# Four transpose banks, rotated running sums and two earlier weight requests in a decoder block's feed-forward part

## The chip, the core and the metric

The kernel runs on one core of a Trainium2 chip. The metric is device time in microseconds (us) for one execution; the median of three runs of the kernel before is 844.78 us. Engines are named as in the profile: PE (TensorE, matmuls and transposes), ACT (ScalarE), DVE (VectorE), POOL (GpSimd) and SP (SyncE, which only issues DMA transfers here). Each works through its own list of instructions in the order written; semaphores hold an instruction back until what it reads is ready and what it overwrites has been read. POOL has little to do in the part that is changed: two tiny powers and one load.

## The reference, cut to what matters

One decoder layer on 512 positions of width 1024. The part that the change touches is the end of sub-layer 1, the norm that follows, and the SwiGLU feed-forward part (`D_FF` = 2816):

```python
x = x + gate1 * (merged @ w_out)

h2 = rms_norm(x, norm2_g) * (1.0 + scale2) + shift2
f_g, f_u = jnp.split(h2 @ w_ffn_in, 2, axis=-1)
x = x + gate2 * ((jax.nn.silu(f_g) * f_u) @ w_ffn_out)
return rms_norm(x, final_norm_g)
```

## The kernel before, in words

Everything is float32 and split in two: a value is kept as a rounded part `hi` and a remainder `lo`, and a product is three matmuls (`mm3`, lines 51 to 55: hi*hi, hi*lo, lo*hi). So each block of weights that comes from HBM into a buffer called `raw` is copied by ACT to `hi` (line 110) and then subtracted by DVE to give `lo` (line 114); when DVE is done, the `raw` buffer is free and SP may ask for the next block. There are three `raw` buffers (`RAWB`), used in turn. All instructions are written out by hand in one order; no scheduler moves them.

**The output projection** (lines 1240 to 1278). The 512 positions are worked on in two halves of 256 (`half`). Half 0 goes through the eight blocks of `w_out`, `n_` = 0 to 7, with sums in PSUM banks 4 to 7; half 1 goes through the same blocks with sums in banks 0 to 3. When a 512-column half of the width is complete (`kts[0] == 6`, at `n_` = 3 and `n_` = 7 in half 1), `resid` (line 1101) multiplies by the gate, adds the residual (DVE) and sums the squares (ACT). Beside half 1's matmuls stand the norm of half 0 and the preparation of the first feed-forward blocks `WF0[0]` to `WF0[3]` (the first two for the gate, the last two for the up projection), which are asked for by `ensure`.

**The norm's transposes** (`norm2_T`, line 1130). The normed rows `xn` are transposed by PE, four 128x128 transposes into one PSUM bank (tile `x2T`, line 1152). One bank holds two 128-wide slices `kt` of the width, a pair `k2`; a half has four pairs. Each slice is read out of the bank twice, once by ACT (line 1159, gives `hi`) and once by DVE or ACT (lines 1162 and 1164, gives the unrounded `hf`), and DVE subtracts the two (line 1165, gives `lo`). The readers of one bank take turns. The pairs use banks 4 and 7 in turn. For half 0 the pairs (0, 1) are transposed after `n_` = 2 and the pairs (2, 3) after `n_` = 3; for half 1 two pairs stand behind each of the two blocks of the up projection of half 0 (line 1476).

**The first feed-forward groups** (lines 1464 to 1487) are plain products into banks 0 to 3 (tile `pf`): for half 0 the gate and then the up block, for half 1 the same. Beside them DVE forms differences of the normed halves (`t_diff`, line 1319) and ACT and DVE split these (`t_split`, line 1327).

**The half groups** (lines 1496 to 1568). The other groups are computed by a Strassen-like scheme with seven products instead of eight. A step `q` (from -2 to 17) handles half a group, gate for even `q` and up for odd. Its weights come in two blocks, asked for by `s_issue(q)` (line 1174) and worked into sums, `hi` and `lo` by `s_prep(q)` (four pairs of an ACT and a DVE part, `a0`,`d0` to `a3`,`d3`, lines 1205 to 1236). The weights of `q` are prepared while PE computes `q - 1`; those of `q` = -2 are prepared in the output projection (line 1269) and around it. `sprod` (line 1490) is one of the seven products, 12 matmuls of 256 columns, and adds to one of four PSUM tiles `R[0]` to `R[3]`. Between products ACT copies one running sum into the next bank (`R[1]` from `R[0]`, line 1529; `R[2]` from `R[1]`, line 1540) or out to `ps` (lines 1536 and 1547). Even `q` use banks 4 to 7 and odd `q` banks 0 to 3.

**The last product** (`zprod`, line 1591) does the same on the output weights with 512 columns, in the banks of the list `ZB`.

SP's list of transfers around the change is: the blocks of `w_out`, the four blocks `WF0`, then the two blocks of each half group from `q` = -2 on. Which buffer a block gets decides how long SP waits before it asks; and as SP's list is in order, a transfer that waits holds up all behind it.

Of the kernel before, what the change touches and what calls it, by code (L numbers as in the profile page):

```python
# [9 lines left out]
F32 = mybir.dt.float32  # L10
# [18 lines left out]
def block_kernel(ctx: ExitStack, tc: tile.TileContext, x, positions, w_ada, b_ada, w_in,  # L29
# [12 lines left out]
    def bank(k, name="bank"):  # L42
        return psum.tile([128, 512], F32, name=name, tag=f"b{k}", bufs=1)

    def f(ap):
        return ap.bitcast(F32)
# [11 lines left out]
    stream, wseq, chunk = [], [], {}  # L58
# [58 lines left out]
    def ensure(upto):  # L117
        upto = min(upto, len(stream) - 1, st["limit"] - 1)
        while True:
            for i in range(st["prep"], min(st["prep"] + 16, len(stream), st["limit"])):  # L120
                if "raw" in stream[i]:
                    continue
                if room(i):
                    issue(i)
                elif stream[i]["kind"] == "w" or not stream[i]["mid"]:
                    break
            if st["prep"] > upto:
                break
            prep(st["prep"])
            st["prep"] += 1  # L130

    def room(i):
        e = stream[i]
        pend = stream[st["prep"]:i]
        if e["kind"] == "m" and e["early"]:
            return sum(p["kind"] == "m" for p in pend) < 8
        if e["kind"] == "m" and e["mid"]:
            return all(p["kind"] == "w" for p in pend) and len(pend) <= 1
        return sum(p["kind"] == "w" or not (p["early"] or p["mid"]) for p in pend) < RAWB


    def get(i, ahead=2):
        k = wseq.index(i)
        ensure(wseq[min(k + ahead, len(wseq) - 1)])
        return chunk[i]
# [13 lines left out]
    ffn = []  # L159
# [114 lines left out]
    for i in range(4):  # L274
        t = base.tile([128, D], F32, name=f"x{i}", tag=f"X{i}", bufs=1)
# [30 lines left out]

    R = mid.tile([128, 6, 128], F32, name="ropes", tag="A1", bufs=1)
    posf, ang, nh, nl, t0 = R[:, 0], R[:, 1], R[:, 2], R[:, 3], R[:, 4]
    chain = []
# [168 lines left out]
    for kt in range(8):  # L478
        hi, lo = chunk[W1[kt]]
# [327 lines left out]
    for g in range(4):  # L807
        pb = [bank2(b, "pav") for b in nbanks()]
        for i in W_AV[g]:
# [10 lines left out]
            hi, lo = get(i)  # L820
# [306 lines left out]
            else:  # L1127
                V.tensor_scalar(xn[tk], xt[tk], r2[:, tk:tk + 1], None, op0=OP.mult)

    def norm2_T(half, kts, after=()):  # L1130
        if kts[0]:
            pass
        elif half == 0:
            for kh in range(2):
                t = ffn[0].tile([128, 4, 256], F32, name="h2f", tag=f"F{kh}", bufs=1)
                for j in range(4):
                    h2f[kh * 4 + j, 0] = t[:, j]
                h2f["t", kh, 0] = [t[:, 0:2], t[:, 2:4]]
        else:
            for kh in range(2):  # L1140
                h2f["t", kh, 1] = []
                for q in range(2):
                    t = base.tile([128, 2, 256], F32, name="h2f", tag=f"S1_{kh * 2 + q}", bufs=1)
                    h2f["t", kh, 1].append(t)
                    for j in range(2):
                        h2f[kh * 4 + q * 2 + j, 1] = t[:, j]
        for k2 in kts:
            p = bank(7 if k2 % 2 else 4, "x2T")
            for k in range(2):
                kt = k2 * 2 + k  # L1150
                for e in range(2):
                    T.transpose(p[:, k * 256 + e * 128:k * 256 + (e + 1) * 128],
                                xn[2 * half + e][:, kt * 128:(kt + 1) * 128], ident)
            for k in range(2):
                kt = k2 * 2 + k
                g, s = Gc[:, 1, kt:kt + 1], Gc[:, 1, 8 + kt:9 + kt]
                src = p[:, k * 256:(k + 1) * 256]
                hi, lo = (t[:, kt % 4] for t in HB[kt // 4, half])
                A.activation(hi, src, AF.Identity, scale=g, bias=s)  # L1159
                hf = h2f[kt, half]  # L1160
                if kt % 4 == 3 or half and kt % 2:
                    A.activation(hf, src, AF.Identity, scale=g, bias=s)  # L1162
                else:
                    V.tensor_scalar(hf, src, g, s, op0=OP.mult, op1=OP.add)  # L1164
                V.tensor_sub(lo, hf, f(hi))
            if k2 in after:
                for fn in after[k2]:
                    fn()


    NQ = 18
# [2 lines left out]
    def s_issue(q):  # L1174
        if q >= NQ:
            return
        c0 = (2 + q // 2) * 256 + (DFF if q % 2 else 0)
        sraw[q] = []
        for kh in range(2):
            if q > 0 and q % 2 and kh:  # L1180
                t = ffn[0].tile([128, 4, 2, 128], F32, name="raw", tag="F0", bufs=1)
            else:
                t = base.tile([128, 4, 2, 128], F32, name="raw", tag="raw", bufs=RAWB)
            SY.dma_start(t.rearrange("p j a n -> p j (a n)"),
                         w_ffn_in[kh * 512:(kh + 1) * 512, c0:c0 + 256].rearrange("(j p) n -> p j n", p=128))
            sraw[q].append(t)
# [53 lines left out]
    WF0 = W_F[0] + W_F[1]  # L1240
    OORD = (W_O, [W_O[n_] for n_ in (0, 2, 4, 5, 1, 3, 6, 7)])
    for half in range(2):
        po = {}
        for n_, (h, i) in enumerate(OORD[half]):
            if half == 0:
                wch[i] = get(i, min(4, 7 - n_))
            hi, lo = wch[i]
            kts = stream[i]["kts"]
            if kts[0] == 0:
                po[h] = [bank(4 - 4 * half + 2 * h + e, "po") for e in range(2)]  # L1250
            for e in range(2):
                opt_a_mm(po[h][e], 2 * half + e, hi, lo, kts, mT, 8)
            if kts[0] == 6:
                for e in range(2):
                    resid(po[h][e], 512 * h, 512, h, 2 * half + e, gate_b[1])
            if half == 1:
                if n_ == 1:
                    for e in range(2):
                        row_rstd(e)
                    norm2_x(0)  # L1260
                    ensure(WF0[1])
                if n_ in (2, 3):
                    norm2_T(0, (0, 1) if n_ == 2 else (2, 3))
                if n_ in (3, 4):
                    ensure(WF0[n_ - 1])
                if n_ == 4:
                    s_issue(-2)
                if n_ == 6:
                    pre = s_prep(-2)
                    for fn in pre[0]:  # L1270
                        fn()
# [47 lines left out]
    def t_diff():  # L1319
        for q in range(2):  # L1320
            b11, b21, b12, b22 = (h2f["t", kh, th][q] for th in range(2) for kh in range(2))
            V.tensor_sub(b11, b12, b11)
            V.tensor_sub(b12, b22, b12)
            V.tensor_sub(b22, b22, b11)
            V.tensor_sub(b21, b21, b22)
# [139 lines left out]
    for half in range(2):  # L1465
        o = slice(half * 256, (half + 1) * 256)
        for w in range(2):
            for ci, i in enumerate(W_F[w]):
                hi, lo = chunk[i]
                for j, kt in enumerate(stream[i]["kts"]):  # L1470
                    for m in range(2):
                        cc = slice(m * 128, (m + 1) * 128)
                        mm3(pf[w][m][:, o], (hi[:, j, cc], lo[:, j, cc]), tuple(t[:, j] for t in HB[ci, half]),
                            kt + half == 0, kt == 7, skip_group_check=True)
                if half == 0 and w == 1:
                    norm2_T(1, (2 * ci, 2 * ci + 1), {3: pre[3]})
            if half == 0 and w == 1:
                s_issue(-1)
                t_diff()
            if half == 1:  # L1480
                if w == 0:
                    EV[w](0)(pf[w])
                t_split(w + 1)
                if w == 1:
                    t_split(3)
                    EV[w](0)(pf[w])
                    t_split(4)
# [8 lines left out]
    for q in range(-2, NQ):  # L1496
# [3 lines left out]
        pre = s_prep(q + 1)  # L1500
        half_of = lambda t, e: tuple(v[:, :, e] for v in t)
        S2_, S1_, A12, A22, S4_, S3_ = (half_of(d[k], e) for k in "CBD" for e in range(2))
        R = [bank(k + 4 * (q % 2 == 0), "R")[:, :256] for k in range(4)]
        ps = [ffn[0].tile([128, 256], F32, name="ps", tag="rt", bufs=2) for _ in range(2)]
        if q >= NQ - 2:
            z_issue(("B11", "B12")[q - NQ + 2])
# [20 lines left out]
        pre[0][0]()  # L1527
        sprod(R[0], d["A"], HB[0, 0], True)
        A.activation(R[1], R[0], AF.Copy)  # L1529
        pre[0][1]()  # L1530
        while left:
            left.pop(0)()
        if q == NQ - 1:
            z_issue("B21")
        sprod(R[3], S1_, TB[1], True)
        A.activation(ps[0], R[3], AF.Copy)
        pre[1][0]()
# [48 lines left out]
            q.dma_start(out[tk * 128:(tk + 1) * 128, c], xo[tk][:, c])  # L1586


    Z, ZB = {}, ((4, 7), (5, 6), (1, 2), (0, 3))

    def zprod(k, ka, kw, start):
        if start:
# [83 lines left out]
    for h in range(2):  # L1676
# [4 lines left out]
        for n_, i in enumerate(ids[:-3] if h else ids):  # L1681
            kts = stream[i]["kts"]
            if h == 0:
                g_split(2 * n_ + 2)
            hi, lo = get(i)
# [91 lines left out]
```

## Time and profile before

| what | value |
|---|---|
| time, median of three runs (range) | 844.78 us (844.73 to 845.04) |
| profiled execution: its own time | 845.55 us |
| profiled execution: span from first to last instruction | 843.4 us |
| granted TensorE clock, mean | 0.997 |
| DVE busy in the span | 668.2 us (79%) |
| ACT busy in the span | 403.7 us (48%) |
| POOL busy in the span | 118.3 us (14%) |
| HBM read | 105.9 MB, 128 GB/s over the span |

Positions are given in us from the start of the span. The part around the change runs from about 470 (end of the output projection) to 532 (the second half group). In the profile an instruction is named by engine, source line and tile: "PE x2T L1152" is a transpose, "DVE h L1165" the subtraction that makes the `lo` part of a normed slice, "ACT wx L110" the copy of a feed-forward block to `hi`, "DVE raw L1212" the first sum over the weights of a half group, "PE R" a product of a half group. Busy time of PE is not a measure of what it could do, since its matmuls overlap; its idle time is.

### The profile page before, as it was taken

What the parts mean: (1) busy time and instruction counts of PE and PEld (TensorE: products, weight loads), DVE (VectorE), ACT (ScalarE), POOL (GpSimd) and SP (SyncE); (2) the same over time, 40 slices, a digit from 0 to 9 for tenths busy, and PEclk for the clock granted to TensorE, in tenths of its full rate; (3) what the DMA queues carried; (4) which work ended last, traced back from release to release, by engine and by line L of the source; (5) the groups of instructions that cost most, each with busy time, mean ns of one, the idle gap of its engine ahead of it and who ended that gap; (6) DMA issues with size and microseconds to landing.
All of it is one profiled execution on the core that took longest, in us unless ns stands there. A gap on an engine that the chain in (4) does not pass through costs nothing. (4 is left out here: it accounts for less than half of the span.)

```text
span 843.4 us, 12878 instructions
## 1 busy us (share of the span) xinstructions
PE 826.0 (98%) x4992; PEld 734.1 (87%) x4992; DVE 668.2 (79%) x1157; ACT 403.7 (48%) x706; POOL 118.3 (14%) x105
## 2 busy tenths in 40 slices
PE   7999999999999999999999989999999999999996
PEld 6788989988888888988888789999999999888885
DVE  7978799788899548886766678889999888985635
ACT  6664445332332226666333456555555555573322
POOL 2060022353344411002210000000000000000001
PEclk9999999999999999999999999999999999999998
DMA  9972362432345641036544130445553334143212
GB/s 297 300 198 68 98 199 77 126 89 86 109 144 197 197 152 51 26 114 236 175 149 150 51 100 26 127 152 162 168 163 108 100 100 146 56 141 99 85 50 100
DMA packets 95677, 109.09 MB, mean 129 GB/s; under 512 B 5617, under 2 KB 76273, under 8 KB 95617
## 3 DMA queue, kind: packets, MB, share of 16 engines
q1 hardware_dynamic: 92512, 101.37, 39.3%
q0 software_dynamic: 2384, 6.10, 2.0%
q8 instruction: 39, 0.64, 0.3%
q10 hardware_dynamic: 720, 0.82, 0.3%
q14 instruction: 22, 0.17, 0.1%
HBM read 105.90 MB, written 2.10 MB: 128 GB/s over the span
## 5 line engine op out<-in xcount | busy, mean ns | idle before, releaser
L110 ACT ACTIVATE hi<-raw 128x1024 fp32r<-128x1024 f32 (+2 forms) x83 | 85.6, 1035 | 107.2 <-PE pfo L55 35.4
L114 POOL TENSOR_TENSOR lo<-raw,hi 128x1024 fp32r<-128x1024 f32 x33 | 83.1, 2522 | 213.2 <-ACT hi L110 194.8
L114 DVE TENSOR_TENSOR lo<-raw,hi 128x1024 fp32r<-128x1024 f32 (+2 forms) x43 | 53.3, 1243 | 50.8 <-ACT hi L110 50.7
L53 PE MATMUL pb<-h,hi 128*128 128x512 f32 x192 | 76.5, 398 | 0.0
L55 PE MATMUL pb<-h,lo 128*128 128x512 f32 x192 | 75.8, 395 | 0.0
L54 PE MATMUL pb<-hl,hi 128*128 128x512 f32 x192 | 75.8, 395 | 0.0
L55 PE MATMUL pfo<-hi,gs 128*128 128x512 f32 (+1 forms) x126 | 46.5, 369 | 0.0
L54 PE MATMUL pfo<-lo,gs 128*128 128x512 f32 (+1 forms) x126 | 46.5, 369 | 0.0
L53 PE MATMUL pfo<-hi,gs 128*128 128x512 f32 (+1 forms) x126 | 46.4, 368 | 0.0
L53 PE MATMUL R<-tb,sx 128*128 128x256 f32 x160 | 45.3, 283 | 0.5 <-ACT R L1529 0.5
L53 PE MATMUL R<-tb,hi 128*128 128x256 f32 x160 | 45.1, 282 | 0.8 <-ACT ps L1547 0.7
L54 PE MATMUL R<-tb,sx 128*128 128x256 f32 x160 | 45.1, 282 | 0.0
L55 PE MATMUL R<-tb,sx 128*128 128x256 f32 x160 | 45.1, 282 | 0.0
L55 PE MATMUL R<-tb,lo 128*128 128x256 f32 x160 | 44.9, 280 | 0.0
L54 PE MATMUL R<-tb,hi 128*128 128x256 f32 x160 | 44.7, 279 | 0.0
L55 PEld LDWEIGHTS pb<-h,lo 128*128 128x128 f32 x192 | 36.0, 188 | 8.7
L54 PEld LDWEIGHTS pb<-hl,hi 128*128 128x128 f32 x192 | 36.1, 188 | 8.3
L53 PEld LDWEIGHTS pb<-h,hi 128*128 128x128 f32 x192 | 36.1, 188 | 8.2
L175 DVE SCALAR_TENSOR_TENSOR acc<-mraw,cols,acc 128x512 f32<-128x512 f32 x38 | 31.4, 826 | 9.4 <-DMA mraw<-in_w_ada_dram 8.6
L54 PE MATMUL pav<-lo,h 128*128 128x256 f32 x128 | 35.8, 280 | 0.0
L55 PE MATMUL pav<-hi,hl 128*128 128x256 f32 x128 | 35.8, 280 | 0.0
L53 PE MATMUL pav<-hi,h 128*128 128x256 f32 x128 | 35.8, 280 | 0.0
(376 smaller groups left out, 2655.3 us busy)
## 6 DMA issues: line engine op xcount, KB each, us to landing
raw<-in_w_ffn_in_dram SPq DMA_DIRECT2D x44, 512.0 KB, 4.1
raw<-in_w_in_dram SPq DMA_DIRECT2D x40, 512.0 KB, 3.8
mraw<-in_w_ada_dram SPq DMA_DIRECT2D x22, 512.0 KB, 3.9
raw<-in_w_ffn_out_dram SPq DMA_DIRECT2D x17, 512.0 KB, 3.8
s<-in_w_ada_dram SPq DMA_DIRECT2D x30, 256.0 KB, 5.5
raw<-in_w_ada_dram SPq DMA_DIRECT2D x10, 512.0 KB, 4.8
raw<-in_w_proj_a_dram SPq DMA_DIRECT2D x8, 512.0 KB, 4.7
raw<-in_w_proj_b_dram SPq DMA_DIRECT2D x8, 512.0 KB, 3.6
```

Source lines behind the costliest of these rows:

```text
L53: T.matmul(o, wh, rh, start=start, stop=False, **kw)
L54: T.matmul(o, wh, rlo, start=False, stop=False, **kw)
L55: T.matmul(o, wlo, rh, start=False, stop=stop, **kw)
L110: A.activation(hi[:, :m], e["raw"][:, :m], AF.Copy)
L114: e["lo"].tensor_sub(lo[:, :m], e["raw"][:, :m], f(hi[:, :m]))
L175: V.scalar_tensor_tensor(o, w, cs[:, j:j + 1], o, op0=OP.mult, op1=OP.add)
```

## The change

- `norm2_T` uses four banks, 4 + `k2`, and has lost the `after` argument.
- Half 0: all four pairs are transposed after `n_` = 2. The block `WF0[2]` is converted by ACT between pair 1 and pair 2, and its `lo` part by DVE between pair 2 and pair 3; the first two blocks of half group -2 are asked for there. `WF0[3]` follows after `n_` = 3, behind that step's `resid`.
- Half 1: all four pairs are transposed after the first of the two up blocks; the last part of the preparation of half group -2 (`pre[3]`) stands behind them.
- The second block of half group -1 goes into tile `E5`, which holds the first gate block until half 1 has used it, and no longer into a `raw` buffer. So the two blocks of half group 0 fall on `raw` buffers that come free sooner. Its issue is written behind the gate products of half 1.
- The running sums `R` use the banks 4, 1, 0, 7 for even `q` and 5, 2, 3, 6 for odd `q`; `ZB` is changed to match. Which sums share a bank with which earlier reader stays the same between half groups; for `q` = -2 and -1 the banks of `pf` and `x2T` come in instead.

The instructions are the same in number, except that PE's transposes stand in two runs of sixteen instead of four runs of eight.

```diff
-    def norm2_T(half, kts, after=()):
+    def norm2_T(half, kts):
...
-            p = bank(7 if k2 % 2 else 4, "x2T")
+            p = bank(4 + k2, "x2T")
...
-            if k2 in after:
-                for fn in after[k2]:
-                    fn()
...
-            if q > 0 and q % 2 and kh:
-                t = ffn[0].tile([128, 4, 2, 128], F32, name="raw", tag="F0", bufs=1)
+            if q % 2 and kh:
+                t = ffn[0].tile([128, 4, 2, 128], F32, name="raw", tag="F0" if q > 0 else "E5", bufs=1)
...
-                if n_ in (2, 3):
-                    norm2_T(0, (0, 1) if n_ == 2 else (2, 3))
-                if n_ in (3, 4):
-                    ensure(WF0[n_ - 1])
-                if n_ == 4:
+                if n_ == 2:
+                    stream[WF0[2]]["lo"] = "later"
+                    norm2_T(0, (0, 1))
+                    ensure(WF0[2])
+                    norm2_T(0, (2,))
+                    stream[WF0[2]]["do"]()
                     s_issue(-2)
+                    norm2_T(0, (3,))
+                if n_ == 3:
+                    ensure(WF0[3])
...
-                if half == 0 and w == 1:
-                    norm2_T(1, (2 * ci, 2 * ci + 1), {3: pre[3]})
+                if half == 0 and w == 1 and ci == 0:
+                    norm2_T(1, range(4))
+                    for fn in pre[3]:
+                        fn()
             if half == 0 and w == 1:
+                t_diff()
+            if half == 1 and w == 0:
                 s_issue(-1)
-                t_diff()
...
-        R = [bank(k + 4 * (q % 2 == 0), "R")[:, :256] for k in range(4)]
+        R = [bank(k, "R")[:, :256] for k in ((4, 1, 0, 7), (5, 2, 3, 6))[q % 2]]
...
-    Z, ZB = {}, ((4, 7), (5, 6), (1, 2), (0, 3))
+    Z, ZB = {}, ((4, 7), (0, 1), (2, 3), (5, 6))
```

## The prediction, made before the run

> **What bounds the kernel now.** First the list of PE's own waits, from 470 us on: engine, line, releaser, then total us, times, longest.
>
> ```profile
> PE x2T L1152 <- ACT h2f L1162: 2.1, 2, 1.4
> PE x2T L1152 <- ACT xn L1126: 1.1, 1, 1.1
> PE R L53 <- ACT ps L1547: 0.7, 1, 0.7
> PE R L53 <- ACT R L1529: 0.5, 1, 0.5
> ```
>
> These are all: 4.4 us. Next the table of stretches (busy us of PE, PEld, DVE, ACT, POOL, then the granted clock).
>
> ```profile
> 506.00:517.00 11.00, 11.00 (x96) 11.00 (x95) 8.91 (x15) 8.00 (x13) 0.00 (x0) 1.00 0.16 49
> 517.00:532.00 15.00, 13.71 (x112) 13.11 (x111) 13.41 (x20) 9.12 (x20) 0.00 (x0) 1.00 0.14 39
> 532.00:832.00 300.00, 300.00 (x2086) 279.65 (x2086) 240.78 (x315) 155.45 (x259) 1.65 (x3) 1.00 0.37 116
> ```
>
> From 532 to 832 PE has no idle time at a clock of 1.00; there a change of order can win nothing, and every us by which PE gets to 532 sooner is a us off the end. So the question is what decides when PE gets there. The list of waits names the last releaser only; the chain of work, asked for 476 to 533, names all (start, us, what).
>
> ```profile
> 486.62 1.24 DVE wx L114
> 487.88 3.46 DMA raw<-in_w_ffn_in_dram
> ...
> 491.43 0.69 DVE raw L1212
> ...
> 531.39 0.37 ACT R L1529
> ...
> 531.81 0.39 PE R L53
> ```
>
> The reader is to see that between 487 and 531.81 PE is not in this chain. DVE subtracts block `WF0[3]`, with the last `raw` buffer; only then SP asks for the second block of half group -2, which takes 3.46 us to land while DVE stands before L1212; from 491.43 on everything is DVE and ACT in their written order (second norm, transposes' evacuation, `t_diff`, `t_split`, the weights of half group -1), 531.81 - 491.43 = 40.38 us without a break. PE's 4.4 us of waits are the shadow of this chain.
>
> **What the change does to the chain's head.** Of the many moved instructions the sum needs one thing: when does DVE reach the first weight sum (L1212 before)? I write out the queues of ACT and DVE anew, with steps from start to start out of the time line.
>
> ```profile
> 476.99 0.56 ACT L1162 ACTIVATE h2f<-x2T,Gc 128x256 f32<-128x256 f32 x1
> ...
> 480.74 0.63 ACT L1106 ACTIVATE rt<-xr 128x512 f32<-128x512 f32 x1 [0.60 <-ACT rt L1106]
> 481.28 0.19 ACT L1106 ACTIVATION_READ_ACCUMULATOR rt<-xr 128x1 f32 x1
> 481.37 0.55 ACT L1159 ACTIVATE h<-x2T,Gc 128x256 fp32r<-128x256 f32 x1
> ...
> 485.08 0.56 ACT L1162 ACTIVATE h2f<-x2T,Gc 128x256 f32<-128x256 f32 x1
> 485.53 2.01 ACT L110 ACTIVATE wx<-raw 128x1024 fp32r<-128x1024 f32 x2
> 487.43 0.63 ACT L1209 ACTIVATE sa<-raw 128x512 fp32r<-128x512 f32 x1
> ...
> 520.34 1.06 ACT L1218 ACTIVATE sx<-raw 128x1024 fp32r<-128x1024 f32 x1
> ```
>
> ```profile
> 477.58 0.43 DVE L1165 TENSOR_TENSOR h<-h2f,h 128x256 fp32r<-128x256 f32 x1 [0.63 <-ACT h2f L1162]
> 477.92 0.68 DVE L1104 TENSOR_TENSOR rt<-po,gate1b 128x512 f32<-128x512 f32 x1
> ...
> 485.67 0.42 DVE L1165 TENSOR_TENSOR h<-h2f,h 128x256 fp32r<-128x256 f32 x1 [0.63 <-ACT h2f L1162]
> 486.62 2.36 DVE L114 TENSOR_TENSOR wx<-raw,wx 128x1024 fp32r<-128x1024 f32 x2 [0.53 <-ACT wx L110]
> ...
> 500.35 1.23 DVE L1229 TENSOR_TENSOR lo<-raw,hi 128x1024 fp32r<-128x1024 f32 x1
> 501.49 0.54 DVE L1164 TENSOR_SCALAR h2f<-x2T,Gc 128x256 f32<-128x256 f32 x1
> ```
>
> Up to ACT's last read of the second transposed pair (476.99) nothing differs. From there, in the new order:
> - ACT converts `WF0[2]`: 0.45 later (485.08 to 485.53); its next instruction 0.95 after that (half of 485.53 to 487.43): 478.39.
> - Pairs 2 and 3 are read out, now without a wait for PE. Before, from ACT's first read to DVE's last subtraction: 481.37 to 485.67, 4.30. Between them DVE now has the subtraction of `WF0[2]`, a 1024-wide step of 1.14 (500.35 to 501.49): 483.83. To the next independent step 0.34 (477.58 to 477.92): 484.17.
> - `resid` of the first columns, from DVE's first multiply to ACT's second square 2.82 (477.92 to 480.74): 486.99. ACT free 0.63 later (to 481.37): 487.62.
> - ACT converts `WF0[3]`, DVE starts to subtract it 1.09 later (485.53 to 486.62): 488.71; one step of 1.14: **489.85**.
>
> That is 491.43 - 489.85 = **1.58 us** sooner. This is also the price of the sooner request: the second block of half group -2 is asked for when DVE is through with `WF0[2]`, before pair 3 is read, so before 483; with the 3.46 above it lands before 486.5, over 3 us ahead of its reader. The 3.46 us of waiting go, but most of them are filled by work that DVE did earlier before: what is late next is DVE's own queue.
>
> **What of the rest lies beside other work.** From L1212 on DVE and ACT have the same instructions in the same order, so the 40.38 us stay and all of them move by 1.58: the second `xn`, the evacuation, the two waits in the `R` stage. The `resid` behind needs PE's last output product; its multiply now falls at about 491.9, and PE has that product when three blocks of 24 feed-forward matmuls (0.115 each by the row 506:517, 8.3 us) are still to come before this row:
>
> ```profile
> 498.04 0.27 PE L1152 MATMUL x2T<-cst,xn 128*128 128x128 f32 x1
> 499.42 0.98 PE L1152 MATMUL x2T<-cst,xn 128*128 128x128 f32 x7 [1.10 <-ACT xn L1126]
> ```
>
> so by about 489.8, less what PE gains before: no wait. The four banks take away PE's 2.1 us for the bank (L1162), and PE would be early for the chain by 2.1 + 1.1 and more. It then waits elsewhere: half 1's products need slices that ACT and DVE have not read out yet. I expect the 2.1 to come back mostly as many small waits of `pf` for DVE L1165, and the wait for `xn` to stay (0.3 to 1.1), since `xn` moves by 1.58 and PE by the 0.7 to 1.0 of its first bank wait. Worth at the end: nothing. If that cover were gone (DVE ahead of PE), the four banks would count in full; that is a rival below.
>
> Two sides of the evacuation, told by the list of ACT's waits:
>
> ```profile
> ACT h L1159 <- DVE h2f L1164: 5.9, 7, 1.3
> ```
>
> ACT waits for DVE's read of the same bank. [...]
>
> The second block of half group -1 is asked for *later* than before. SP's issues were:
>
> ```profile
> 501.60 0.37 SPq L1184 DMA_DIRECT2D raw<-in_w_ffn_in_dram x1
> 511.58 0.37 SPq L1184 DMA_DIRECT2D raw<-in_w_ffn_in_dram x1
> 528.62 2.14 SPq L1184 DMA_DIRECT2D raw<-in_w_ffn_in_dram x3
> ```
>
> 501.60 was that block; now SP stands until PE has used the first gate block for half 1, by the working above at about 506, and lands near 509.5. Its first reader, ACT L1218 at 520.34, is then due at 518.8: 9 us of cover. The blocks of half group 0 (511.58 and 528.62) follow right behind, the second some 18 us sooner than before; DVE's work for half group 0 gains room that PE, without a wait there, cannot use. Cost and gain: 0.
>
> Banks of `R` and `ZB`: 0. In half group -2 `R[1]` and `R[2]` now stand in the gate's banks, read by ACT's Silu which precedes on ACT's own list; in -1 they stand in the up banks, read by DVE ten us ahead. Later the two sets alternate as before. Whether a bank makes PE quicker or slower the trace doesn't show by itself; both sets are in the row of 532 to 832 without a gap, and I keep 0.4 us on both sides for it.
>
> **Sum.** The profiled execution, 845.55 (span 843.4), would become 845.55 - 1.58 = 843.97; the median of the runs shown, 844.78, lies 0.77 below that execution and by the same term becomes **843.2**. The parts of the sum that could be off: each of nine steps by some 0.05, one DMA by 0.2, so 842.6 to 843.8.
>
> **Rivals.**
> - *PE is the bound.* [...] For it: the 2.1 us are named as a bank wait. Against: the chain has no PE in it for 44 us. 8%.
> - *The head doesn't move.* If one more wait turns up in the rewritten queue (ACT's conversion ahead of pair 2, or `resid` behind all four pairs), DVE gets to L1212 at 491.4 as before: 844.4 to 845.0. Against: each step is a row of the same work. 9%.
> - *Slower: SP stands at `E5`.* One transfer at the head of SP's list waits for PE, and three half groups' blocks behind it. From 9 us of delay its reader is late, and each us more adds one; it takes 9 + 1.6 + 1.7 = 12.3 us in place of 3.5 to be slower by over 0.2%: 846.5 and more. Against: the landing in the chain took 3.46 us. 3%.
>
> **How the numbers follow.** What a measurement of this kernel can tell from no change is about 0.2%, 1.7 us: below 843.1 is faster, and the forecast of 843.2 lies just inside. Forecast 80%, of which three eighths fall below 843.1 (0.30) and the rest above (0.50); the first rival is faster (0.08), the second the same (0.09), the third slower (0.03). Faster 0.38, same 0.59, slower 0.03. The range 842.2 to 844.4 leaves out the first and third rival and half of the second, some 16%.
>
> **What would show it.** DVE reaches the first weight sum (L1209 in the new file) near 489.9, by subtraction of `WF0[3]` and not by a DMA; the stretch from there to the last wait of `R` is again 40.4 us; PE's wait for L1162 is gone and waits of `pf` for DVE L1165 are new; the two waits of `R` stay at 0.5 to 0.8. If instead the first sum comes later than 491, or PE's waits shrink below 2 us in all, the chain was not what I took it for. A pace of PE after 532 other than 300 us for the same 2086 matmuls would mean that the banks count.

## The result, and the profile of the changed kernel

| | before | changed |
|---|---|---|
| median of 15 runs (range) | 845.04 us (844.73 to 845.42) | 843.20 us (842.89 to 843.60) |
| profiled execution: its own time, span | 845.55, 843.4 | 843.06, 841.1 |
| granted TensorE clock, mean | 0.997 | 0.998 |

The ratio is 0.9978, with a 95% interval of 0.997 to 0.9986: 1.84 us faster, the interval going from 1.2 to 2.5 us.

**The chain of work** of the changed kernel, from 476 to 533 (start, us, what), in the places that the prediction showed of before:

```profile
487.06 0.96 ACT wx L110
...
488.05 0.04 DVE wx L114
488.08 1.11 issue
489.19 0.69 DVE raw L1209
...
529.09 0.37 ACT R L1533
529.46 0.04 issue
529.50 0.38 PE R L53
```

The transfer has left the chain. In front of the first weight sum (now L1209) stands DVE's own subtraction of `WF0[3]` (L114; the chain gives the rest of its time as "issue") behind ACT's copy of it; from that sum to PE's product the chain runs as before, 529.50 - 489.19 = 40.31 us (before 40.38).

**The rewritten head**, in the time lines of ACT and of DVE:

```profile
472.60 0.56 ACT L1159 ACTIVATE h<-x2T,Gc 128x256 fp32r<-128x256 f32 x1 [2.08 <-PE x2T L1152]
...
476.33 0.56 ACT L1162 ACTIVATE h2f<-x2T,Gc 128x256 f32<-128x256 f32 x1
476.78 1.06 ACT L110 ACTIVATE wx<-raw 128x1024 fp32r<-128x1024 f32 x1
477.73 0.56 ACT L1159 ACTIVATE h<-x2T,Gc 128x256 fp32r<-128x256 f32 x1
...
486.34 0.63 ACT L1106 ACTIVATE rt<-xr 128x512 f32<-128x512 f32 x1 [0.60 <-ACT rt L1106]
486.88 0.19 ACT L1106 ACTIVATION_READ_ACCUMULATOR rt<-xr 128x1 f32 x1
486.97 1.05 ACT L110 ACTIVATE wx<-raw 128x1024 fp32r<-128x1024 f32 x1
```

```profile
483.18 0.43 DVE L1165 TENSOR_TENSOR h<-h2f,h 128x256 fp32r<-128x256 f32 x1 [0.63 <-ACT h2f L1162]
483.52 0.68 DVE L1104 TENSOR_TENSOR rt<-po,gate1b 128x512 f32<-128x512 f32 x1
...
488.05 1.22 DVE L114 TENSOR_TENSOR wx<-raw,wx 128x1024 fp32r<-128x1024 f32 x1 [1.79 <-ACT wx L110]
489.19 0.69 DVE L1209 TENSOR_TENSOR raw<-raw 128x512 f32<-128x512 f32 x1
```

The reader is to lay the prediction's nine steps beside these starts: 0.45 (476.33 to 476.78), 0.95, then 5.45 to DVE's last subtraction (4.30 and 1.14), 0.34, 2.82 (483.52 to 486.34), 0.63, 1.08, 1.14. Their sum is 489.19 - 476.33 = 12.86 us, the sum of the steps in the prediction. The two executions stand 0.66 us apart already at 476.99 and 476.33, ahead of anything that was moved, so the difference at PE's product (531.81 - 529.50 = 2.31) consists of those 0.66, of 1.58 from the head, and of 0.07.

**PE's waits** from 470 on, and the row of the table of stretches behind them (PE, PEld, DVE, ACT, POOL, clock):

```profile
PE R L53 <- ACT R L1533: 1.2, 2, 0.7
PE R L53 <- ACT ps L1551: 0.8, 1, 0.8
PE x2T L1152 <- ACT xn L1126: 0.6, 1, 0.6
```

```profile
532.00:832.00 300.00, 300.00 (x2088) 279.53 (x2087) 239.91 (x315) 153.71 (x257) 1.65 (x3) 1.00 0.37 115
```

The wait for the bank (L1162, 2.1 us) is gone. Part of it has come back between matmuls, where the list of waits names nothing; PE's time line shows three places like this one:

```profile
507.25 0.28 PE L53 MATMUL pf<-h,wx 128*128 128x256 f32 x1
507.61 0.39 PE L54 MATMUL pf<-h,wx 128*128 128x256 f32 x1
507.83 0.28 PE L55 MATMUL pf<-h,wx 128*128 128x256 f32 x1
```

L54 is the first matmul of a slice that reads `lo`. It starts 0.36 us after L53 instead of 0.12, and the next one 0.22 after it: 0.35 us lost here, 0.93 at the three places (505.25, 506.21 and 507.25). From 532 to 832 PE keeps its pace, 2088 matmuls in 300 us against 2086.

**SP's issue** of the second block of half group -2, and the time to landing of that transfer and the next:

```profile
481.70 0.37 SPq L1181 DMA_DIRECT2D raw<-in_w_ffn_in_dram  x1
```

```profile
DMA to landing us min/median/max: 3.6/3.6/3.6
```

It lands at about 485.3, 3.9 us ahead of its reader. **ACT's wait** for DVE in the evacuation is still there, from 470 on (us in all, times, longest; before 6.5, 8, 1.3):

```profile
ACT h L1159 <- DVE h2f L1164: 7.6, 8, 2.2
```

### The profile page after: what moved, and what is told of

It is laid out like the page before. It is cut to its first block, busy times and chain, and to the rows that moved or that the text cites. A ratio compares the mean times of both kernels' runs of the same rounds, so it can differ in the third digit from the quotient of the medians.

```text
span 841.1 us, 12872 instructions
## 1 busy us (share of the span) xinstructions
PE 825.5 (98%) x4992; PEld 733.7 (87%) x4992; DVE 668.2 (79%) x1157; ACT 403.5 (48%) x706; POOL 118.3 (14%) x105
## 5 line engine op out<-in xcount | busy, mean ns | idle before, releaser
L114 POOL TENSOR_TENSOR lo<-raw,hi 128x1024 fp32r<-128x1024 f32 x33 | 83.1, 2521 | 213.3 <-ACT hi L110 207.7
L114 DVE TENSOR_TENSOR lo<-raw,hi 128x1024 fp32r<-128x1024 f32 (+2 forms) x43 | 53.3, 1243 | 50.8 <-ACT hi L110 50.6
L53 PE MATMUL pb<-h,hi 128*128 128x512 f32 x192 | 76.4, 398 | 0.0
L54 PE MATMUL pb<-hl,hi 128*128 128x512 f32 x192 | 75.8, 395 | 0.0
L53 PE MATMUL R<-tb,hi 128*128 128x256 f32 x160 | 45.0, 281 | 1.5 <-ACT ps L1551 0.8
L54 PE MATMUL pfo<-lo,gs 128*128 128x512 f32 (+1 forms) x126 | 46.4, 368 | 0.0
L53 PE MATMUL pfo<-hi,gs 128*128 128x512 f32 (+1 forms) x126 | 46.4, 368 | 0.0
L53 PE MATMUL R<-tb,sx 128*128 128x256 f32 x160 | 45.3, 283 | 0.5 <-ACT R L1533 0.5
L54 PE MATMUL R<-tb,sx 128*128 128x256 f32 x160 | 45.1, 282 | 0.0
L54 PE MATMUL R<-tb,hi 128*128 128x256 f32 x160 | 44.7, 280 | 0.0
L54 PEld LDWEIGHTS pb<-hl,hi 128*128 128x128 f32 x192 | 36.0, 188 | 8.4
L53 PEld LDWEIGHTS pb<-h,hi 128*128 128x128 f32 x192 | 36.0, 188 | 8.3
L54 PE MATMUL pav<-lo,h 128*128 128x256 f32 x128 | 35.8, 279 | 0.0
L53 PE MATMUL pav<-hi,h 128*128 128x256 f32 x128 | 35.8, 279 | 0.0
```

Of the source, the lines that this page charges most:

```text
L53: T.matmul(o, wh, rh, start=start, stop=False, **kw)
L54: T.matmul(o, wh, rlo, start=False, stop=False, **kw)
L114: e["lo"].tensor_sub(lo[:, :m], e["raw"][:, :m], f(hi[:, :m]))
```

## The experiments

The theory: the time is set by one chain of DVE's and ACT's instructions, from the evacuation of half 0 to PE's product of half group -1, and only what shortens that chain counts. Rivals: PE's bank waits are what counts; the new buffer or the new banks of `R` count.

Two of the first kernels, "banks_only" and "head_only", give another result than the reference; instructions and their order are what the text says, so their times bear on the argument. They keep the old banks of `R`, and in half group -2 the sums that ACT copies into `R[1]` and `R[2]` then stand in banks that held transposes. That the result differs for this reason is my guess, and no run tests it. It would give the change's rotation of `R` and `ZB` its reason: two banks per set that held no transposes.

### The banks alone, in the kernel before

```diff
-            p = bank(7 if k2 % 2 else 4, "x2T")
+            p = bank(4 + k2, "x2T")
```

> The kernel before with four transpose banks (4 + k2) in both halves and nothing else. If the chain of ACT and DVE decides: PE's wait for L1162 (2.1 us) goes, the first weight sum L1212 stays at its place behind the 3.46 us transfer, and the time stays that of before (845.0, within 0.3). If PE's bank wait decides: 2 us faster, 843.0.

Measured: 844.73 us against 844.77, ratio 1.0 (0.9992 to 1.0009). PE's list of waits:

```profile
PE R L53 <- ACT R L1529: 1.2, 2, 0.7
PE x2T L1152 <- ACT xn L1126: 1.1, 1, 1.1
PE R L53 <- ACT ps L1547: 0.8, 1, 0.8
PE pf L53 <- DVE rt L1104: 0.6, 1, 0.6
```

The 2.1 us wait for a bank is gone, and nothing is gained. From first weight sum to PE's product it is 40.38 us as before (490.75 to 531.13).

### The head alone

```diff
-            p = bank(7 if k2 % 2 else 4, "x2T")
+            p = bank(7 if k2 % 2 else 4, "x2T") if half else bank(4 + k2, "x2T")
...
-                if n_ in (2, 3):
-                    norm2_T(0, (0, 1) if n_ == 2 else (2, 3))
-                if n_ in (3, 4):
-                    ensure(WF0[n_ - 1])
-                if n_ == 4:
+                if n_ == 2:
+                    stream[WF0[2]]["lo"] = "later"
+                    norm2_T(0, (0, 1))
+                    ensure(WF0[2])
+                    norm2_T(0, (2,))
+                    stream[WF0[2]]["do"]()
                     s_issue(-2)
+                    norm2_T(0, (3,))
+                if n_ == 3:
+                    ensure(WF0[3])
```

> The kernel before with the new order of half 0 alone (four banks there, WF0[2] between the pairs, first request of half group -2 there); half 1, E5 and the banks of R and ZB as before. If the chain decides: DVE reaches the first weight sum 12.9 us after ACT's last read of pair 1, as in the changed kernel, and the whole gain is there, 1.6 to 1.8 us. If the four banks of half 1 or the second request matter: at most a part of it, under 0.8 us.

Measured: 843.06 us against 844.77, ratio 0.998 (0.9971 to 0.9989), the whole gain, though half 1 keeps two banks, the old order and PE's bank wait (1.4 us of L1162 in its list). The parts of the head (order, four banks in half 0, the sooner request) were only run together here; "two_banks" below takes the banks away.

### The change without its head

The reverse of the last edit of `n_`, in the changed kernel.

> The changed kernel with the order of half 0 as before; four banks, sixteen transposes in a run in half 1, E5 and the new banks of R and ZB stay. If the chain decides: no gain left, 845.0 within 0.3. If the second half's part or the banks of R matter: 0.8 us or more of the gain stays.

Measured: 844.86 us, ratio 0.9999 (0.9991 to 1.0008). With all else in place nothing is left of the gain. In this kernel the DMA stands in the chain again, ahead of the first sum at 490.84; from there to PE's product it is 40.35 us.

### The change with two banks

```diff
-            p = bank(4 + k2, "x2T")
+            p = bank(7 if k2 % 2 else 4, "x2T")
```

> The changed kernel with banks 4 and 7 in turn, as before. If four banks are only needed so that the new order can be: PE, whose transposes of pairs 2 and 3 stand ahead of the rest of the output projection, waits about 4 us for the banks there and passes the delay on to resid and the second norm, so slower than before by about 1 us (846). If the banks don't matter for the order either: 843.2 as with four.

Measured: 848.91 us (846.88 to 850.8), ratio 1.0047 (1.0035 to 1.006): slower by 4.1 us than before and by some 5.7 than the change. I had expected about 846. In the profiled execution (846.88), the table of stretches and PE's time line:

```profile
475.00:480.00 5.00, 3.75 (x14) 2.93 (x13) 3.12 (x8) 3.44 (x6) 0.00 (x0) 0.66 0.11 39
```

```profile
471.51 1.04 PE L1152 MATMUL x2T<-cst,xn 128*128 128x128 f32 x8
474.62 0.63 PE L1152 MATMUL x2T<-cst,xn 128*128 128x128 f32 x4 [2.07 <-DVE h2f L1164]
476.49 1.06 PE L1152 MATMUL x2T<-cst,xn 128*128 128x128 f32 x4 [1.25 <-ACT h2f L1162]
...
478.21 0.63 PE L55 MATMUL po<-wx,ml 128*128 128x512 f32 x1
478.63 0.63 PE L53 MATMUL po<-wx,mh 128*128 128x512 f32 x1
479.06 0.63 PE L54 MATMUL po<-wx,mh 128*128 128x512 f32 x1
```

All sixteen transposes now stand in one run, so with two banks PE waits for the evacuation, 2.07 and 1.25 us in half 0, and in half 1 twice more, 3.3 us in all. After the two holes in half 0 the granted clock of the stretch is 0.66 instead of 1.00, and the 512-wide matmuls start 0.43 us apart from 477.78 to 479.91 (478.63 to 479.06, for one), up to 471.51 and from 480.20 on 0.23; the stretches on both sides, 470 to 475 and 480 to 485, have a clock of 1.00. That second loss I had not counted. From 472.55 to 476.49 PE had done nothing but four transposes of 0.63 us in all; that the low clock follows from these two holes is my reading, and what decides when it falls and for how long is not shown. The other runs take up to 4 us more than the profiled one, and their granted clock is lower: 0.996 at 846.88 and 847.63 us, 0.993 at 848.36 and 849.46, 0.989 at 850.42 and 850.80. So the spread goes with the clock; why it differs from run to run is not shown.

The head of DVE's chain is not what suffers: its first weight sum stands at 488.75, 12.87 us behind ACT's last read of pair 1 (475.88), as with four banks. But the chain of work now runs through PE from 476.49 to 501.70 and again from 506.07 on: here PE is the bound. So the four banks give nothing by themselves, and yet the new order needs them. How the loss divides between the two halves no run separates.

### The new banks of the sums, and the transfer into E5

"new_r" is the kernel before with the new banks of `R` and `ZB`; "no_e5" is the changed kernel with the old condition on the buffer:

```diff
-            if q % 2 and kh:
+            if q > 0 and q % 2 and kh:
```

> The kernel before with the new banks of the running sums R and of ZB, and nothing else. If the chain decides and a bank is as quick as another: the time of before, 844.8 within 0.3. If the banks of R make PE quicker: up to 0.4 us less, seen as fewer than 300 us for the same matmuls behind 532.

> The changed kernel with the second block of half group -1 back in a raw buffer, so that SP does not wait for PE there and the blocks of half group 0 are asked for as late as before. If the chain decides: 843.1 as the changed kernel, since the blocks have 9 us of cover either way. If this request carries part of the gain: 0.3 to 1 us of it goes.

Measured: 844.78 against 844.78, ratio 1.0 (0.9991 to 1.0009), and 842.93, ratio 0.9978 (0.997 to 0.9987), the same as the change's. Neither part counts.

### One DVE instruction twice, and sixteen transposes twice

Two probes of who is the bound, both in the changed kernel: the subtraction of `WF0[2]` done twice on DVE, and the transposes of half 1 done twice on PE.

```diff
-                    stream[WF0[2]]["do"]()
+                    for _ in range(2):
+                        stream[WF0[2]]["do"]()
```

```diff
-            for k in range(2):
+            for k in [0, 1] * (1 + half):
                 kt = k2 * 2 + k
```

> The changed kernel with DVE's subtraction of WF0[2] done twice (the second gives the same values again). If the chain of DVE and ACT decides: one for one, 1.15 to 1.25 us later than the changed kernel at the first weight sum and at the end, 844.3. If PE decides: the step lies 15 us ahead of PE's use of that block and costs nothing, 843.1.

> The changed kernel with half 1's sixteen transposes done twice over (the same values again): 1.6 us more work for PE. If the chain decides: PE's waits shrink by the 1.6 us and the end stays, 843.1. If PE decides: 1.6 us later, 844.7.

Measured: with DVE's step twice 844.32, ratio 0.9995 (0.9986 to 1.0004). That is 1.12 us over the 843.20 of the change, and 1.39 over the 842.93 of "no_e5" from the same set of runs. In the trace the doubled step takes 2.40 us (480.17 to 482.57) instead of 1.13 (480.42 to 481.55), and the first weight sum stands 14.13 us behind ACT's last read of pair 1 (476.08 to 490.21) instead of 12.86: 1.27 us for 1.27. With PE's transposes twice 842.96, ratio 0.9979 (0.9971 to 0.9988): some 1.6 us more work on PE cost nothing. From first weight sum to PE's product it is 40.34 us (490.21 to 530.55) and 40.36 us (488.96 to 529.32). This is the plainest answer to the first rival: in this stretch a us of DVE counts whole, and 1.6 us of PE not at all.

### Work of DVE's chain on POOL

If DVE's list is the bound, work taken off it should count in full. Three kernels, all the changed one: "pool_lo" moves the subtraction of `WF0[3]` to POOL, "pool_tdiff" four of the eight subtractions of `t_diff`, "pool_both" both.

```diff
+                    stream[WF0[3]]["lo"] = P
...
-        for q in range(2):
+        for q, E in enumerate((P, V)):
...
-            V.tensor_sub(b11, b12, b11)
+            E.tensor_sub(b11, b12, b11)
...
```

> The changed kernel with the subtraction of WF0[3] on POOL in place of DVE. POOL takes 2.5 us for such a tile by the page, but has nothing else then. If the chain of DVE and ACT decides: DVE goes from resid straight to the weight sums, its second one (L1210) waits only for ACT's copy and starts about 1.2 us sooner than in the changed kernel; 841.9 to 842.0. If the chain is not what decides, or POOL slows DVE down beside it: 843.1 or later.

> The changed kernel with four of the eight differences of the normed halves (those of the first of the two column groups) on POOL. If the chain decides: DVE's list is shorter by four steps of 0.7 us, 2.8 us, of which PE's waits of 4.7 us in this stretch can take all: 840.3. If POOL needs over 2 us for each 512-wide step, t_split waits for POOL and most of it is lost: 842 to 843.

> Both moves to POOL at once. If the chain decides and the two terms add: 1.2 + 2.8 = 4.0 us less than the changed kernel, 839.1, with PE's waits in the stretch down to about 1 us. If PE takes over as the bound before that: no less than pool_tdiff alone, 840.3.

Measured, against 844.95: 843.65, ratio 0.9986 (0.9977 to 0.9994); 841.68, ratio 0.9962 (0.995 to 0.9975); 841.96, ratio 0.9964 (0.9951 to 0.9978). All three are well short of what was expected if the chain decides (841.9 to 842.0, 840.3 and 839.1), and "pool_lo" loses about 0.5 us against the change. (The 2.5 us expected for POOL's tile are before's: 33 subtractions of 128x1024 on POOL at 2522 ns on average.) In the time line of DVE and then of POOL in "pool_lo":

```profile
488.49 2.48 DVE L1210 TENSOR_TENSOR sa<-raw,sa 128x512 fp32r<-128x512 f32 x1 [1.71 <-ACT sa L1206]
491.01 0.69 DVE L1211 TENSOR_TENSOR raw<-raw 128x512 f32<-128x512 f32 x1
```

```profile
488.02 2.41 POOL L114 TENSOR_TENSOR wx<-raw,wx 128x1024 fp32r<-128x1024 f32 x1 [20.68 <-ACT wx L110]
```

This DVE subtraction of 512 columns takes 2.48 us beside POOL's, 0.69 in the changed kernel, and it ends after POOL's has (490.97 against 490.43). DVE's first sum came 3 us sooner (486.10), but then DVE waited 1.71 us for ACT's copy, and the second sum took 1.79 us longer. In "pool_tdiff", where POOL has subtractions from 504.94 to 509.26:

```profile
505.29 0.55 DVE L1164 TENSOR_SCALAR h2f<-x2T,Gc 128x256 f32<-128x256 f32 x1
505.87 0.81 DVE L1165 TENSOR_TENSOR h<-h2f,h 128x256 fp32r<-128x256 f32 x1
506.93 1.19 DVE L1165 TENSOR_TENSOR h<-h2f,h 128x256 fp32r<-128x256 f32 x1 [0.24 <-ACT h2f L1162]
508.04 2.30 DVE L1233 TENSOR_TENSOR lo<-raw,hi 128x1024 fp32r<-128x1024 f32 x1
```

The read of PSUM with one tensor keeps its time (0.55, in the changed kernel 0.54); the subtractions with two inputs in SBUF go from 0.43 to 0.81 and 1.19, and from 1.23 to 2.30. What holds them up beside POOL no run shows; of the three expectations only that of "pool_lo" had named a slower DVE. "pool_tdiff" keeps 1.5 us of the 2.9 us that I had expected; that these are the stretches in which DVE waited for ACT anyway or read PSUM is my reading of the time line, with no run of its own.

### The four banks used: two pairs read out in turn

What the runs leave over is ACT and DVE waiting for each other in the evacuation, where both read one bank in turn (ACT for DVE 7.6 us, 8 times, in the changed kernel). With four banks two pairs can be read in turn:

```diff
+        ps = {}
         for k2 in kts:
-            p = bank(4 + k2, "x2T")
+            p = ps[k2] = bank(4 + k2, "x2T")
...
+        step = 2
+        for i in range(0, len(kts), step):
             for k in range(2):
...
+                for k2 in kts[i:i + step]:
...
-                    norm2_T(0, (0, 1))
+                    norm2_T(0, (0, 1, 2, 3))
                     ensure(WF0[2])
-                    norm2_T(0, (2,))
                     stream[WF0[2]]["do"]()
                     s_issue(-2)
-                    norm2_T(0, (3,))
```

The loop over `kts` now only transposes; the reading is in the new loops.

> The changed kernel, with its four banks used for the one thing that two could not give: within each half the transposes of two pairs stand in two banks before their slices are read, and the slices are read out in turn (pair a's first, pair b's first, pair a's second, pair b's second), so that ScalarE can read one bank while VectorE reads the other; in half 0 VectorE's subtraction of WF0[2] then comes behind all four pairs. If the chain is VectorE's and ScalarE's turns, as the runs so far say: in the changed kernel a pair of half 1 takes 2.09 us (504.90 - 502.81), four take 8.4, with ScalarE waiting 0.61 us at each step for VectorE's read. Read in turn, two pairs need what the busier engine has to do: VectorE two h2f of 0.54 and four subtractions of 0.43 less the overlap, about 2.8 to 3.0 us, so 2.4 us less in half 1, and 1 to 2 us less in half 0, whose waits of ScalarE are of the same kind. All of that leaves the end, up to the 2.6 us of PE's listed waits and the unlisted small ones: 839 to 840.5. If the two engines do not read different banks side by side, or PE is the bound by now: 843.2, as the changed kernel. The list of ScalarE's waits for VectorE's h2f (7.6 us, 8 times) must fall below 3 us in the first case and stay in the second.

Measured: **839.28 us** (838.84 to 839.51) against 844.83, ratio 0.9933 (0.992 to 0.9947): 5.5 us faster than before and 3.7 to 3.9 faster than the change (by the two gains, and by the two medians), inside the expectation. ACT's wait, and all that is left of PE's list from 470 on:

```profile
ACT h L1163 <- DVE h2f L1168: 1.4, 6, 0.4
```

```profile
PE R L53 <- ACT R L1535: 0.3, 1, 0.3
```

ACT and DVE read side by side, each in its own bank (time lines of ACT and of DVE):

```profile
498.90 0.56 ACT L1166 ACTIVATE h2f<-x2T,Gc 128x256 f32<-128x256 f32 x1
```

```profile
498.78 0.54 DVE L1168 TENSOR_SCALAR h2f<-x2T,Gc 128x256 f32<-128x256 f32 x1
```

Where the time went, leg by leg (us; starts from the two kernels' time lines):

| leg | change | in turn | difference |
|---|---|---|---|
| ACT's first read of half 0 to the first weight sum | 16.59 (472.60 to 489.19) | 14.00 (472.97 to 486.97) | -2.59 |
| on to DVE's first read of half 1 | 10.05 (to 499.24) | 10.89 (to 497.86) | +0.84 |
| on to ACT's L1230 (L1234) behind the evacuation | 7.75 (to 506.99) | 5.42 (to 503.28) | -2.33 |
| on to PE's product | 22.51 (to 529.50) | 22.53 (to 525.81) | +0.02 |

In half 0 the subtraction of `WF0[2]` has moved behind all four pairs too, so only the third leg, of half 1, shows the reading in turn by itself. That four banks are needed for it is not shown either: two pairs could be read in turn from two banks in the old order, and no run tries that.

The second leg shows the next bound. In the chain of work PE's matmuls now stand without a break ahead of the evacuation of half 1:

```profile
496.55 0.12 PE pf L54
496.67 0.12 PE pf L55
496.79 0.45 PE x2T L1153 x4
497.24 0.02 issue
497.26 0.57 ACT h L1163
```

ACT and DVE are early there and wait for PE's transposes; after that the chain is theirs again, up to the product.

## Why the prediction was right

It was 843.2 in a range of 842.2 to 844.4; 843.20 was measured. By its steps:

- **PE's 4.4 us are the shadow of a DVE and ACT chain of 40.38 us.** Shown: 40.38, 40.35, 40.31, 40.34 and 40.36 us in five kernels above, while PE had fewer bank waits, more work or DVE started later. Only where half 1 was read out with two banks under the new head ("head_only", 488.85 to 529.50) were they 40.65. In "two_banks" the chain is PE's, so the 40 us hold only while PE is ahead. The rival that PE is the bound (840.4 if all of its 4.4 us went) falls with "banks_only" and "pe_twice".
- **The head gives 1.58 us.** Right in the trace, by "head_only" (1.71 in the medians) and "no_head" (0) also as cause. The hundredth is luck: from ACT's last read of pair 1 to the first weight sum it is 14.44 us before, 14.46, 14.52 and 14.57 in "banks_only", "new_r" and "no_head", which keep the old head, and 12.86 in the change. That makes 1.58 to 1.71. Over the same leg as in the table above, from ACT's first read of half 0 to the first weight sum, before takes 491.43 - 473.26 = 18.17 (row below, before's time line of ACT) and the change 16.59.

```profile
473.26 0.56 ACT L1159 ACTIVATE h<-x2T,Gc 128x256 fp32r<-128x256 f32 x1 [2.09 <-PE x2T L1152]
```

- **The request before 483, the block before 486.5.** 481.70 and about 485.3. The sooner request did what I said, and what was late next was DVE's own list: of 3.46 us of DMA in the chain 1.58 came off the end.
- **The four banks are worth nothing at the end.** Right ("banks_only"), but where the 2.1 us reappear I had partly wrong: I named small waits of `pf`, and there are 0.93 us of them; the waits in the `R` stage, which I let stay at 0.5 to 0.8 each, have grown in number, from 1.2 to 2.0 us in all. And my working didn't see that the new order costs some 5.7 us without them.
- **E5 costs nothing.** SP's issue was at 504.73 (I wrote about 506), with 4.0 us to landing far ahead of its reader; "no_e5" shows that the buffer gains nothing either. The rival that SP stands there falls.
- **Banks of `R` and `ZB`: 0.** "new_r".
- **The turns of ACT and DVE in a bank stay.** The sum takes this for granted, and no run shows whether two engines could read one bank side by side; measured is that ACT's wait stayed (7.6 us, 8 times). Had the turns of half 1 gone, four of the seven waits in before's list, 5.9 x 4/7 = 3.4 us would be the estimate; reading two banks in turn got 2.33 there.
- **The sum.** The profiled execution came out at 843.06 where I had 843.97; 0.66 of that stood already ahead of the first moved instruction. The 843.20 was worked out from a median before of 844.78, and the 15 runs gave 845.04. The median's agreement to the hundredth is therefore luck of some tenths: by the medians the gain is 1.84, interval 1.2 to 2.5, and 1.58 lies inside it.
- **The border.** By the ratio (0.22%) the change lies just beyond the 0.2% that I called measurable, by the time that I wrote for it (843.1) just inside; I had given 0.38 to "faster" and 0.59 to "within". A forecast of 0.19% beside a border of 0.2% is an even chance by its own working, and I leaned on it too much.

## What to carry to other kernels

When PE's list of waits names a bank, ask the chain of work before adding banks: here the bank wait hid behind a chain of two other engines, so four banks in the old order gave 0, and a reading order that let the two engines read different banks at once gave 3.7 to 3.9 us more. Doubling one instruction on each suspected engine (1.1 to 1.4 us for DVE's, 0 for PE's) told the bound here more surely than the list of waits. Work moved from DVE to POOL gave less than it took off DVE's list (1.5 of 2.9 us, and once a loss of 0.5), as DVE's instructions with two inputs in SBUF were slower beside it (2.48 us instead of 0.69, 2.30 instead of 1.23).

## What the runs showed of the hardware that was not expected

- Two holes of PE of 2.07 and 1.25 us with only four transposes between them were followed by matmuls 0.43 us apart instead of 0.23, in a stretch of 5 us with a granted clock of 0.66 instead of 1.00 ("two_banks").
- A DVE subtraction with two SBUF inputs took 2.48 us instead of 0.69 beside a POOL subtraction of 2.41 us ("pool_lo"); beside POOL subtractions of 1.47 and 1.35 us a DVE read of PSUM took 0.55, without them 0.54 ("pool_tdiff").
- After six waits in the changed kernel PE's second matmul started 0.22 or 0.23 us after the first instead of 0.12, so that each of them cost PE 0.10 to 0.11 us more than the wait (505.52, 506.55, 507.61, and the listed waits at 517.78, 524.49 and 529.50).
